# Sparse attention: scores of a head pair by 64-row halves, keys stored without the zeros

## The chip, the cores and the metric

The kernel runs on one core of one Trainium2 chip. The metric is the device time of one execution in microseconds. The kernel before takes 1622.97 us (median of 3 runs, 1621.4 to 1623.26).

## The reference

The program computes two stacked blocks of a small network on 256 tokens of width 1024, in fp32. The first block has an HGRN2 mixer, an attention mixer and two feed-forward layers; the second has a short convolution, a sparse attention mixer and four feed-forward layers. The change lies in the sparse attention alone. Cut to what matters there:

```
q = rmsnorm(x @ w_q)                        # 16 heads of 64, in 4 groups of 4 heads
k_cmp, v_cmp, k_sel, v_sel, k_win, v_win    # one head of 64 per group and branch
for each group g, each of its heads h:
    o_cmp = softmax(q[h] k_cmp[g]^T / 8, blocks that end at or before t) v_cmp[g]   # 15 compressed keys
    o_sel = softmax(q[h] k_sel[g]^T / 8, keys <= t) v_sel[g]
    o_win = softmax(q[h] k_win[g]^T / 8, keys <= t) v_win[g]
    out[h] = gate0 * o_cmp + gate1 * o_sel + gate2 * o_win
y = concat(out) @ w_o
```

With 256 tokens every block of 64 is selected and the window of 512 covers everything, so the selected and the window branch are both plain causal attention over 256 keys, with keys and values of their own.

## The kernel before, in words

All large products are split: a weight chunk arrives by DMA in `raw`, ScalarE rounds it to `hi` (`split_one`, L362) and VectorE writes the rest to `lo` (L363); TensorE adds three products per pair (L550, L571, L597). Almost the whole program is this stream of matmuls of 256 columns.

The sparse attention has three parts. `Sparse.__init__` makes the buffers that outlive a stage: GpSimd writes the zeros of `kbd`, `kcbd` and `vcbd` (L1102 to L1106). `project` makes keys and values from the shared projection; `key_t` (L1196) transposes the normalised keys of one branch on TensorE, two banks of PSUM for the two halves of the tokens, and each bank is written to `kbd` in two parts, rows 0 to 63 by ScalarE (L1206) and rows 64 to 127 by VectorE (L1207). `compress` does the compressed keys and ends with two ScalarE instructions into `kcbd` (L1284). `attend` (L1289) is the attention itself.

The queries of one pair of heads stand in 128 partitions: head 0 of the pair in partitions 0 to 63, head 1 in 64 to 127. `kbd` is block diagonal: in rows 0 to 63 the keys stand in the first half of the columns and zeros in the second, in rows 64 to 127 the other way round. One fp32 product over all 128 rows thus gives the scores of both heads side by side. A causal mask is added by one more matmul, identity times mask, in fp32r (one instruction, where an fp32 product is two, each a weight load and a matmul).

`pair(i)` (L1327), for eight pairs, has three stages, separated by `yield`. Stage 1 takes four PSUM banks of the pool `acc` (it has four in all): `pa` holds the scores of tokens 0 to 127 on the first 128 keys (two branches, two heads: four blocks of 128), `pb` and `pc` those of tokens 128 to 255 on all 256 keys (one branch each, two heads), `pd` the compressed scores (four blocks of 64). VectorE then takes the row maxima (four `tensor_reduce`, L1351), ScalarE the exponentials with row sums (twelve, L1354), in the order `pa`, `pb`, `pc`, `pd`, and VectorE the reciprocals, the gates and three products (L1357 to L1368). Stage 2 transposes the result (14 transposes, L1377 to L1386, pool `wk`) and copies it out. Stage 3 multiplies by the values (L1390 to L1398): one product on the whole array, then eight on halves of 64 columns, the two heads in turn, and splits the output into `zh`, `zl` (L1400).

`attend` interleaves `queries(g)`, stages of `pair(i)` and `out(k)` (the output projection, which needs all four `acc` banks) by a list written out by hand (L1418 to L1427). `queries(1)` uses two `acc` banks too. The order in which each engine then executes is made when the program is built, from dependences and free buffers: in the trace instructions of several pairs stand mixed on one engine.

Of the kernel before, what the change touches and what calls it, by code (L numbers as in the profile page):

```python
# [271 lines left out]
def nsa_masks():  # L272

    t = np.arange(P)[:, None]
# [3 lines left out]
    return np.concatenate([causal] + [c for c in cmp for _ in range(2)], axis=1).astype(np.float32)  # L278
# [813 lines left out]
class Sparse:  # L1092
    def __init__(self, net, pool):
# [3 lines left out]
        self.kbd = pool.tile([P, 2, 4, 2, T], F32, name="kbd")  # L1097
        self.v = pool.tile([P, 2, 2, T], F32, name="v_sw")
        self.kcbd = pool.tile([P, 4, P], F32, name="kcbd")
        self.vcbd = pool.tile([P, 4, P], F32, name="vcbd")  # L1100
        nc.scalar.dma_start(self.c, net.aps["nsa_c"])
        nc.gpsimd.memset(self.kbd[0:64, :, :, 1, :], 0.0)  # L1102
        nc.gpsimd.memset(self.kbd[64:P, :, :, 0, :], 0.0)
        for t in (self.kcbd, self.vcbd):
            nc.gpsimd.memset(t[0:64, :, 64:P], 0.0)
            nc.gpsimd.memset(t[64:P, :, 0:64], 0.0)  # L1106
# [89 lines left out]
    def key_t(self, s, kn):  # L1196
# [3 lines left out]
        for i in range(2):  # L1200
# [5 lines left out]
            nc.scalar.activation(self.kbd[0:64, br, :, 0, c], ps[0:64], AF.Copy, scale=gain[0:64])  # L1206
            nc.vector.tensor_scalar(self.kbd[64:P, br, :, 1, c], ps[64:P], gain[64:P], None, ALU.mult)  # L1207


    def compress(self):  # L1210
# [8 lines left out]
        for s in range(2):  # L1219
# [69 lines left out]
    def attend(self, norm, post):  # L1289
# [7 lines left out]
        causal = masks[:, :P]  # L1297
# [29 lines left out]
        def pair(i):  # L1327
            g, pr = i // 2, i % 2
            q = q_t[g][:, pr, :]
            pa, pb, pc, pd = [net.acc.tile([P, 512], F32, tag="acc", name=net.name("nl")) for _ in range(4)]  # L1330
            t0, t1 = q[:, 0:P], q[:, P:T]
# [227 lines left out]
```

## Time and profile before

| | |
|---|---|
| median of 3 runs | 1622.97 us (1621.4 to 1623.26) |
| profiled execution, own time | 1622.46 us |
| its span, first to last instruction | 1620.6 us |
| TensorE matmul busy | 1602.0 us, 99% |
| VectorE, ScalarE, GpSimd busy | 1127.2, 853.3, 53.2 us |
| mean granted TensorE clock | 0.999 |

Busy times are those of the profiled execution. A matmul's recorded end is modelled, so the records of matmuls that follow each other overlap: the cost of one is read from the distance between starts, not from its duration. `attend` lies between about 1318 and 1435 us of the span; its tiles in the profile are `nl` (scores; one name for `pa` to `pd`), `nmx` (maxima), `e` (exponentials), `nt` (transposes), `no` (product with the values).

### The profile page before, as it was taken

How to read it: one execution, taken by the hardware profiler on the slowest of the kernel's cores; microseconds unless marked ns; L12 is line 12 of the kernel's file. 1: busy time of each engine (PE TensorE's matmuls, PEld its weight loads, DVE VectorE, ACT ScalarE, POOL GpSimd, SP SyncE). 2: the span in 40 equal slices, each digit the busy share in tenths (PEclk: the TensorE clock that was granted, in tenths of full speed). 3: DMA queues.
4: the chain of work that ended last, by engine and by line, in shares of the span. 5: the costliest groups of instructions: out<-in, count | busy, mean ns of one | idle time of the engine just before them, and what ended most of it. 6: DMA issues, size and time to landing. Idle time of an engine off the chain costs nothing.

```text
span 1620.6 us, 32338 instructions
## 1 busy us (share of the span) xinstructions
PE 1602.0 (99%) x13704; PEld 1574.4 (97%) x13704; DVE 1127.2 (70%) x1657; ACT 853.3 (53%) x1392; POOL 53.2 (3%) x50
## 2 busy tenths in 40 slices
PE   8999999999999999999999999999999999999999
PEld 8999999999999999999999999999999996799999
DVE  6878866676586667866686866668666668776664
ACT  7674544455554446544454544455545557654442
POOL 0000100000000000000000100001000011000000
PEclk9999999999999999999999999999999999999999
DMA  8325455455445544654555555546554641045451
GB/s 311 130 94 183 176 187 204 179 192 190 143 187 182 205 182 157 231 207 184 201 190 186 200 191 194 197 157 234 183 210 181 237 167 49 29 161 208 180 207 51
DMA packets 43565, 289.09 MB, mean 178 GB/s; under 512 B 4851, under 2 KB 7580, under 8 KB 9244
## 3 DMA queue, kind: packets, MB, share of 16 engines
q1 hardware_dynamic: 42784, 286.48, 48.5%
q8 instruction: 107, 1.75, 0.4%
q10 hardware_dynamic: 636, 0.55, 0.1%
q14 instruction: 38, 0.31, 0.1%
HBM read 284.93 MB, written 1.06 MB: 176 GB/s over the span
## 4 chain that ended last, share of the span: by engine, by line
PE 84%; issue 10%; DVE 3%; POOL 1%; ACT 1%; DMA 0%; SPq 0%; DVEq 0%; POOLq 0%; ACTq 0%
PE pj L550 51%; PE dn L597 26%; PE pn L571 3%; PE nl L1332 1%; PE no L1332 1%; POOL hms L1131 1%; DVE lo L363 1%; PE ph L1237 1%; DVE xl L430 0%; POOL r L514 0%; DVE h L617 0%; DMA h<-x_t 0%; DVE e L1368 0%; PE mo L1043 0%; DVE e L466 0%
## 5 line engine op out<-in xcount | busy, mean ns | idle before, releaser
L363 DVE TENSOR_TENSOR lo<-raw,hi 128x1024 fp32r<-128x1024 f32 (+2 forms) x537 | 653.3, 1222 | 276.4 <-ACT hi L362 275.0
L362 ACT ACTIVATE hi<-raw 128x1024 fp32r<-128x1024 f32 (+2 forms) x537 | 562.0, 1055 | 470.9 <-PE pj L550 389.9
L550 PE MATMUL pj<-xh,hi 128*128 128x256 f32 x2656 | 738.7, 278 | 0.1
L550 PE MATMUL pj<-xl,hi 128*128 128x256 f32 x2656 | 735.5, 277 | 0.3 <-DVE xl L430 0.3
L550 PE MATMUL pj<-xh,lo 128*128 128x256 f32 x2656 | 734.9, 277 | 0.1
L550 PEld LDWEIGHTS pj<-xl,hi 128*128 128x128 f32 x2656 | 498.8, 188 | 1.4 <-DVE xl L430 0.8
L550 PEld LDWEIGHTS pj<-xh,hi 128*128 128x128 f32 x2656 | 498.9, 188 | 1.1 <-ACT xh L429 0.5
L550 PEld LDWEIGHTS pj<-xh,lo 128*128 128x128 f32 x2656 | 498.6, 188 | 0.4 <-DVE lo L363 0.3
L597 PE MATMUL dn<-zh,hi 128*128 128x256 f32 x1312 | 363.4, 277 | 0.0
L597 PE MATMUL dn<-zh,lo 128*128 128x256 f32 x1312 | 362.7, 276 | 0.0
L597 PE MATMUL dn<-zl,hi 128*128 128x256 f32 x1312 | 362.6, 276 | 0.0
L597 PEld LDWEIGHTS dn<-zh,hi 128*128 128x128 f32 x1312 | 246.4, 188 | 0.4 <-issue 0.2
L597 PEld LDWEIGHTS dn<-zl,hi 128*128 128x128 f32 x1312 | 246.3, 188 | 0.1
L597 PEld LDWEIGHTS dn<-zh,lo 128*128 128x128 f32 x1312 | 246.3, 188 | 0.0
L434 ACT ACTIVATE zh<-ft 128x256 fp32r<-128x256 f32 x132 | 54.7, 417 | 155.4 <-DVE ft L634 155.4
L631 DVE TENSOR_TENSOR ft<-pj,rbc 128x512 f32<-128x512 f32 x132 | 90.7, 690 | 51.1 <-PE pj L550 50.5
L435 DVE TENSOR_TENSOR zl<-ft,zh 128x256 fp32r<-128x256 f32 x132 | 55.7, 424 | 54.8 <-ACT zh L434 54.8
L571 PE MATMUL pn<-hi,xh 128*128 128x256 f32 (+1 forms) x256 | 73.7, 289 | 1.0 <-DVE e L1143 1.0
L571 PE MATMUL pn<-hi,xl 128*128 128x256 f32 (+1 forms) x256 | 72.9, 285 | 0.0
L571 PE MATMUL pn<-lo,xh 128*128 128x256 f32 (+1 forms) x256 | 72.6, 284 | 0.0
L632 ACT ACTIVATE ft<-ft 128x256 f32<-128x256 f32 x132 | 52.8, 402 | 9.9 <-DVE ft L631 9.7
L634 DVE TENSOR_TENSOR ft<-ft 128x256 f32<-128x256 f32 x132 | 54.9, 418 | 1.3 <-ACT ft L632 1.2
(236 smaller groups left out, 1144.6 us busy)
## 6 DMA issues: line engine op xcount, KB each, us to landing
raw<-wts SPq DMA_DIRECT2D x263, 1024.0 KB, 4.8
raw<-wts SPq DMA_DIRECT2D x4, 1072.0 KB, 5.0
h<-x_t SPq DMA_DIRECT2D x4, 256.0 KB, 4.8
hank<-bias_d SPq DMA_DIRECT2D x1, 1024.0 KB, 8.3
out_dram<-h SPq DMA_DIRECT2D x4, 256.0 KB, 2.1
kk<-lsum SPq DMA_DIRECT2D x1, 576.0 KB, 8.1
raw<-wts SPq DMA_DIRECT2D x2, 256.0 KB, 4.5
raw<-wts SPq DMA_DIRECT2D x1, 512.0 KB, 6.0
```

What stands on the lines that cost most here:

```text
L362: self.nc.scalar.activation(hi[:, p], src[:, p], AF.Copy)
L363: self.nc.vector.tensor_sub(lo[:, p], src[:, p], hi[:, p].bitcast(F32))
L434: self.nc.scalar.activation(hi, src, AF.Copy)
L435: self.nc.vector.tensor_sub(lo, src, hi.bitcast(F32))
L550: nc.tensor.matmul(o, a[:, c:c + P], b[k], start=(k == 0 and m == 0 and q == 0), stop=(k == KT - 1 and q == 2), skip_group_check=True)
L571: nc.tensor.matmul(o, a[k][:, i * P:(i + 1) * P], b[:, kk * ncol:(kk + 1) * ncol], start=(k == 0 and q == 0 and (i == 0 or banks == 2)), s ...
L597: nc.tensor.matmul(o, a[:, c:c + P], x, start=(j == 0 and m == 0 and q == 0), stop=(j == self.n - 1 and q == 2), skip_group_check=True)
L631: nc.vector.tensor_mul(t, ps, state["rb"])
L632: nc.scalar.activation(t[:, :T], t[:, :T], AF.Silu)
L634: nc.vector.tensor_mul(t[:, :T], t[:, :T], t[:, T:])
L1131: nc.gpsimd.tensor_tensor(ms[:, :n], ms[:, :n], net.nhalf[:, :n], ALU.pow)
L1332: mm = lambda o, a, b, st, sp: nc.tensor.matmul(o, a, b, start=st, stop=sp, skip_group_check=True)
```

## The change

The keys are stored once, in both halves of the partitions, without zeros: `k2[P, 4, 2, T]` (group, branch, key) takes the place of `kbd`, `kc2[P, 4, 64]` that of `kcbd`; the zeros are no longer written. The projection already makes the keys twice (`scaled2`), so one instruction over 128 partitions fills both halves: in `key_t` ScalarE does the first half of the tokens, VectorE the second; in `compress` one ScalarE instruction does both.

In `pair` each product runs over 64 rows of the array, one per head: `u` is the head, `c` its 64 partitions. Each head has banks of its own: `pa[u]` holds tokens 0 to 127 (two branches, 256 columns) and both compressed blocks (2 times 64 columns); `pb[u]` holds tokens 128 to 255 (two branches, 512 columns). The masks follow all products. There are six reductions instead of four, head 0 first; the exponentials keep their order (causal blocks of tokens 0 to 127, of 128 to 255, compressed), which now goes back and forth between the two heads' banks.

```diff
-            for br in range(2):
-                mm(pa[:, br * T:(br + 1) * T], t0, self.kbd[:, br, g, :, 0:P], br == 0, False)
-            mm(pa, identr, causal.unsqueeze(1).to_broadcast([P, 4, P]), False, True)
-            for br, x in enumerate((pb, pc)):
-                mm(x, t1, self.kbd[:, br, g, :, :].rearrange("p a t -> p (a t)"), True, False)
-                mm(x.rearrange("p (a t) -> p a t", a=2)[:, :, P:], identr, causal.unsqueeze(1).to_broadcast([P, 2, P]),
+            for u, c in enumerate(half):
+                mm(pa[u][:, :T], q[c, t0], self.k2[c, g, :, 0:P], True, False)
+            for u, c in enumerate(half):
+                mm(pb[u], q[c, t1], self.k2[c, g, :, :].rearrange("p b t -> p (b t)"), True, False)
+            for i_, t in enumerate((t0, t1)):
+                for u, c in enumerate(half):
+                    mm(pa[u][:, T + i_ * 64:T + i_ * 64 + 64], q[c, t], self.kc2[c, g, :], False, False)
+            for u in range(2):
+                mm(pa[u][:, :384], identr, masks, False, True)
+            for u in range(2):
+                mm(pb[u].rearrange("p (a t) -> p a t", a=2)[:, :, P:], identr, masks[:, :T].rearrange("p (a t) -> p a t", a=2),
                    False, True)
-            mm(pd[:, 0:P], t0, self.kcbd[:, g, :], True, False)
-            mm(pd[:, P:T], t1, self.kcbd[:, g, :], False, False)
-            mm(pd[:, :T], identr, masks[:, P:], False, True)
...
-            for src, c, n in ((pa, 0, 4), (pb, 4, 2), (pc, 6, 2), (pd[:, :T], 8, 4)):
-                nc.vector.tensor_reduce(mx[:, c:c + n], src.rearrange("p (h k) -> p h k", h=n), AX.X, ALU.max,
-                                        negate=True)
+            for u in range(2):
+                for src, c in ((pa[u][:, :T], 0), (pb[u], 4), (pa[u][:, T:384], 8)):
+                    nc.vector.tensor_reduce(mx[:, c + u:c + 4:2], src.rearrange("p (h k) -> p h k", h=2), AX.X, ALU.max,
+                                            negate=True)
...
-            nc.scalar.activation(self.kbd[0:64, br, :, 0, c], ps[0:64], AF.Copy, scale=gain[0:64])
-            nc.vector.tensor_scalar(self.kbd[64:P, br, :, 1, c], ps[64:P], gain[64:P], None, ALU.mult)
+            if i:
+                nc.vector.tensor_scalar(self.k2[:, :, br, c], ps, gain, None, ALU.mult)
+            else:
+                nc.scalar.activation(self.k2[:, :, br, c], ps, AF.Copy, scale=gain)
...
-            for o in (0, 64):
-                nc.scalar.activation(self.kcbd[o:o + 64, :, o:o + 64], pt[o:o + 64, :, o:o + 64], AF.Copy,
-                                     scale=self.col(C_KN)[o:o + 64])
+            nc.scalar.activation(self.kc2, pt[:, :, 0:64], AF.Copy, scale=self.col(C_KN))
```

## Rows read from the trace of the kernel before

**Rows 1.** The page's first lines: the span, and each engine's busy time in us, its share of the span and its instructions.

```profile
span 1620.6 us, 32338 instructions
PE 1602.0 (99%) x13704; PEld 1574.4 (97%) x13704; DVE 1127.2 (70%) x1657; ACT 853.3 (53%) x1392; POOL 53.2 (3%) x50
```

**Rows 2.** Busy times by stretch inside `attend`: from:to in us, its length, then busy us (and instructions) of PE, PEld, DVE, ACT, POOL, the granted clock, the DMA share and GB/s.

```profile
1343.00:1412.00 69.00, 65.93 (x428) 49.00 (x429) 54.31 (x127) 51.65 (x227) 4.12 (x2) 0.98 0.08 30
...
1384.00:1410.00 26.00, 25.74 (x185) 18.46 (x187) 21.66 (x49) 19.41 (x88) 0.00 (x0) 1.00 0.00 1
...
1344.00:1348.00 4.00, 4.00 (x17) 3.39 (x18) 2.41 (x5) 3.27 (x17) 0.00 (x0) 0.58 0.39 166
```

**Rows 3.** The chain that ended last, from 1318 to 1425 us: its shares by line, and one of its pieces (start us, us, what).

```profile
by line: PE nl L1332 15.4%; PE no L1332 12.6%; PE dn L597 10.3%; POOL hms L1131 8.6%; PE pn L571 6.9%; DVE lo L363 5.6%; DVE e L1368 3.9%; PE nt L1377 3.3%; DVE xl L430 3.1%; PE nt L1382 3.0%; issue 2.9%; DVE nmx L1351 2.8%; PE nt L1378 2.7
...
1391.94 3.61 PE nl L1332 x16
```

**Rows 4.** TensorE's timeline over the scores of pair 6, which stand here in one piece: start us, us, engine, line, out<-in, rows*columns of the array, moving operand, how many were merged.

```profile
1391.77 1.03 PE L1332 MATMUL nl<-kbd,qt 128*128 128x256 f32 x4
1392.45 0.58 PE L1332 MATMUL nl<-masks,identr 128*128 128x512 f32 x1
1392.87 1.02 PE L1332 MATMUL nl<-kbd,qt 128*128 128x512 f32 x2
1393.33 0.68 PE L1332 MATMUL nl<-masks,identr 128*128 128x256 f32 x1
1393.85 1.02 PE L1332 MATMUL nl<-kbd,qt 128*128 128x512 f32 x2
1394.30 0.68 PE L1332 MATMUL nl<-masks,identr 128*128 128x256 f32 x1
1394.82 0.61 PE L1332 MATMUL nl<-kcbd,qt 128*128 128x128 f32 x4
1395.18 0.36 PE L1332 MATMUL nl<-masks,identr 128*128 128x256 f32 x1
```

**Rows 5.** The same timeline, just after: one whole product with the values (`no`), and the first row of the next.

```profile
1395.38 0.59 PE L1332 MATMUL no<-yb,vcbd 128*128 128x256 f32 x2
1395.91 0.65 PE L1332 MATMUL no<-ya,v_sw 128*64 128x256 f32 x4
1396.39 0.39 PE L1332 MATMUL no<-yb,v_sw 128*64 128x128 f32 x4
1396.61 0.60 PE L1332 MATMUL no<-ya,v_sw 128*64 128x256 f32 x4
1397.04 0.39 PE L1332 MATMUL no<-yb,v_sw 128*64 128x128 f32 x4
1397.36 0.70 PE L1332 MATMUL no<-yb,vcbd 128*128 128x256 f32 x2
```

**Rows 6.** Groups of VectorE instructions between 1339 and 1420 us, shapes apart: count | busy us, mean ns | idle time before them and what ended it. First the maxima, then the three products.

```profile
L1351 DVE TENSOR_REDUCE nmx<-nl 128x2 f32<-128x512 f32 x16 | 10.6, 675 | 0.4 <-PE nl L1332 0.3
L1351 DVE TENSOR_REDUCE nmx<-nl 128x4 f32<-128x512 f32 x8 | 5.4, 678 | 3.5 <-PE nl L1332 3.3
L1351 DVE TENSOR_REDUCE nmx<-nl 128x4 f32<-128x256 f32 x8 | 3.3, 415 | 0.4 <-PE nl L1332 0.4
...
L1368 DVE TENSOR_TENSOR e<-e,ncf 128x1024 f32<-128x1024 f32 x8 | 9.7, 1217 | 0.0
L1368 DVE TENSOR_TENSOR e<-e,ncf 128x512 f32<-128x512 f32 x8 | 5.5, 684 | 0.0
L1368 DVE TENSOR_TENSOR e<-e,ncf 128x256 f32<-128x256 f32 x8 | 3.3, 417 | 0.0
```

**Rows 7.** ScalarE's timeline: the first and the last of pair 0's twelve exponentials, then the last of pairs 1, 4 and 7.

```profile
1344.73 0.37 ACT L1354 ACTIVATE e<-nl,nmx 128x128 f32<-128x128 f32 x1 [4.21 <-DVE nmx L1351]
...
1348.78 0.37 ACT L1354 ACTIVATE e<-nl,nmx 128x64 f32<-128x64 f32 x1
...
1356.79 0.33 ACT L1354 ACTIVATE e<-nl,nmx 128x64 f32<-128x64 f32 x1
...
1386.95 0.33 ACT L1354 ACTIVATE e<-nl,nmx 128x64 f32<-128x64 f32 x1
...
1411.30 0.35 ACT L1354 ACTIVATE e<-nl,nmx 128x64 f32<-128x64 f32 x1
```

**Rows 8.** TensorE's timeline: the first scores of pair 2 and of pair 5.

```profile
1353.24 0.60 PE L1332 MATMUL nl<-kbd,qt 128*128 128x256 f32 x2
...
1381.11 1.03 PE L1332 MATMUL nl<-kbd,qt 128*128 128x256 f32 x4
```

**Rows 9.** TensorE's timeline: the scores of pair 0 that go to `pc`; in brackets the idle time before and what ended it.

```profile
1343.82 1.30 PE L1332 MATMUL nl<-kbd,qt 128*128 128x512 f32 x2 [1.90 <-DVE qn L1138]
```

**Rows 10.** The instructions that write the keys (duration min/median/max in ns, first and last start in us), a wait of TensorE in that stage (us in total, times, longest), and GpSimd's timeline at the zeros and after them.

```profile
L1206 ACT ACTIVATE kbd<-kt,nsa_c x4: 667/677/683, 1110.9 to 1125.6; 64x512 f32<-64x512 f32 x4
...
L1207 DVE TENSOR_SCALAR kbd<-kt,nsa_c x4: 753/756/757, 1115.0 to 1126.5; 64x512 f32<-64x512 f32 x4
...
PEld pn L571 <- ACT kbd L1206: 1.2, 1, 1.2
...
898.39 1.81 POOL L1102 MEMSET kbd<- 64x2048 f32 x1 [47.91 <-DVE zl L435]
...
906.44 1.31 POOL L466 TENSOR_TENSOR e<-e 128x512 f32<-128x512 f32 x1 [3.01 <-issue]
```

More of the change, by code (lines that the diff above doesn't have):

```diff
@@ L277, in nsa_masks @@
     cmp = [np.where((n < 15) & (16 * n + 31 <= t + P * i), 0.0, NEG) for i in range(2)]
-    return np.concatenate([causal] + [c for c in cmp for _ in range(2)], axis=1).astype(np.float32)
+    return np.concatenate([causal, causal] + cmp, axis=1).astype(np.float32)
 def pack_rel(inputs):
@@ L1096, in __init__ @@
         self.c = pool.tile([P, N_C], F32, name="nsa_c")
-        self.kbd = pool.tile([P, 2, 4, 2, T], F32, name="kbd")
+        self.k2 = pool.tile([P, 4, 2, T], F32, name="k2")
         self.v = pool.tile([P, 2, 2, T], F32, name="v_sw")
-        self.kcbd = pool.tile([P, 4, P], F32, name="kcbd")
+        self.kc2 = pool.tile([P, 4, 64], F32, name="kc2")
         self.vcbd = pool.tile([P, 4, P], F32, name="vcbd")
         nc.scalar.dma_start(self.c, net.aps["nsa_c"])
[L1102 to L1106, printed above, removed]
+        nc.gpsimd.memset(self.vcbd[0:64, :, 64:P], 0.0)
+        nc.gpsimd.memset(self.vcbd[64:P, :, 0:64], 0.0)
         self.hq = pool.tile([P, 1], F32, name="hq")
@@ L1296, in attend @@
         nc.vector.tensor_copy(identr, net.ident)
-        causal = masks[:, :P]
         q_t, gates, z = {}, {}, {}
@@ L1329, in pair @@
             q = q_t[g][:, pr, :]
-            pa, pb, pc, pd = [net.acc.tile([P, 512], F32, tag="acc", name=net.name("nl")) for _ in range(4)]
-            t0, t1 = q[:, 0:P], q[:, P:T]
+            pa = [net.acc.tile([P, 512], F32, tag="acc", name=net.name("nl")) for _ in range(2)]
+            pb = [net.acc.tile([P, 512], F32, tag="acc", name=net.name("nl")) for _ in range(2)]
+            half = [slice(u * 64, u * 64 + 64) for u in range(2)]
+            t0, t1 = slice(0, P), slice(P, T)
             mm = lambda o, a, b, st, sp: nc.tensor.matmul(o, a, b, start=st, stop=sp, skip_group_check=True)
-            for br in range(2):
-                mm(pa[:, br * T:(br + 1) * T], t0, self.kbd[:, br, g, :, 0:P], br == 0, False)
-            mm(pa, identr, causal.unsqueeze(1).to_broadcast([P, 4, P]), False, True)
-            for br, x in enumerate((pb, pc)):
-                mm(x, t1, self.kbd[:, br, g, :, :].rearrange("p a t -> p (a t)"), True, False)
-                mm(x.rearrange("p (a t) -> p a t", a=2)[:, :, P:], identr, causal.unsqueeze(1).to_broadcast([P, 2, P]),
+            for u, c in enumerate(half):
[9 more added lines that the diff above has]
+                mm(pb[u].rearrange("p (a t) -> p a t", a=2)[:, :, P:], identr, masks[:, :T].rearrange("p (a t) -> p a t", a=2),
                    False, True)
-            mm(pd[:, 0:P], t0, self.kcbd[:, g, :], True, False)
-            mm(pd[:, P:T], t1, self.kcbd[:, g, :], False, False)
-            mm(pd[:, :T], identr, masks[:, P:], False, True)
             mx = net.sp.tile([P, 12], F32, tag="nmx", name=net.name("nmx"))
@@ L1346, in pair @@
             xa, xb = net.e4(), net.e4()
-            parts = [(pa[:, j * P:(j + 1) * P], xa[:, j * P:(j + 1) * P]) for j in range(4)]
-            parts += [((pb, pc)[j // 2][:, (j % 2) * T:(j % 2 + 1) * T], xb[:, j * T:(j + 1) * T]) for j in range(4)]
-            parts += [(pd[:, j * 64:(j + 1) * 64], xa[:, 512 + j * 64:512 + (j + 1) * 64]) for j in range(4)]
-            for src, c, n in ((pa, 0, 4), (pb, 4, 2), (pc, 6, 2), (pd[:, :T], 8, 4)):
-                nc.vector.tensor_reduce(mx[:, c:c + n], src.rearrange("p (h k) -> p h k", h=n), AX.X, ALU.max,
-                                        negate=True)
+            parts = [(pa[j % 2][:, (j // 2) * P:(j // 2 + 1) * P], xa[:, j * P:(j + 1) * P]) for j in range(4)]
+            parts += [(pb[j % 2][:, (j // 2) * T:(j // 2 + 1) * T], xb[:, j * T:(j + 1) * T]) for j in range(4)]
+            parts += [(pa[j % 2][:, T + (j // 2) * 64:T + (j // 2 + 1) * 64], xa[:, 512 + j * 64:512 + (j + 1) * 64])
+                      for j in range(4)]
+            for u in range(2):
+                for src, c in ((pa[u][:, :T], 0), (pb[u], 4), (pa[u][:, T:384], 8)):
+                    nc.vector.tensor_reduce(mx[:, c + u:c + 4:2], src.rearrange("p (h k) -> p h k", h=2), AX.X, ALU.max,
+                                            negate=True)
             for j, (src, dst) in enumerate(parts):
```

## The prediction

> **What bounds the kernel now.** I read the page's head first: TensorE is busy 99% of the span, VectorE 70%, ScalarE 53% [rows 1], so only what shortens TensorE's stream, or makes it wait, can count. But a share of the whole span says little of one stage, so I next read busy times by stretch inside the attention [rows 2]. From 1343 to 1412 us, where the eight pairs' scores lie, TensorE is busy 65.93 of 69 us, VectorE 54.31, ScalarE 51.65: TensorE leads, the others are not far behind. From 1384 to 1410 it is 25.74 of 26 against 21.66 and 19.41. The chain of waits over 1318 to 1425 us [rows 3] then says how much of that stretch hangs on the scores: 15.4% of 107 us, that is 16.5 us. As one pair's scores in one piece take 3.61 us [rows 3], eight take 28.9 us; 57% of them stand on the chain. The rest of the chain is other TensorE work and, up to about 1384, maxima, products and the query scaling on VectorE and GpSimd.
>
> **The scores on TensorE.** From the starts in [rows 4, 5]: two fp32 products of 256 columns and a mask of 512 take 1.10 us (1391.77 to 1392.87), a product of 512 and a mask of 256 take 0.98 (twice), two products of 128 and a mask of 256 take 0.56; together 3.61. An fp32 product is two instructions. The first two differ by 256 mask columns, so these cost 0.12 us, and an fp32 instruction of 256 columns costs (1.10 - 0.24)/4 = 0.215 us. After the change the number of columns is the same: products of 2 x 256, 2 x 512 and 4 x 64 against 2 x 256, 2 x 512 and 2 x 128. Were the halves to run one after the other nothing would be won. All hangs on two halves running side by side.
>
> The trace has no product on 64 rows. The nearest is that on 64 columns, the product with the values [rows 5]. One takes 1.98 us (1395.38 to 1397.36). One after the other its instructions would take 2 x 0.215 on the whole array and 8 x 0.215 + 8 x 0.108 on halves, 3.01 us; with the halves side by side 0.43 + 1.29 = 1.72. So they do run side by side, and the 0.26 us left over is what going to halves and back costs. I take the same for rows. Then a pair's scores cost: tokens 0 to 127, 2 x 0.215 = 0.43; tokens 128 to 255, 0.86; the compressed ones 0.22 if columns decide and 0.36 if the weight load does (four instructions with 128-column weights take 1394.82 to 1395.18), I take 0.29; masks 1280 columns, 0.60; the change of shape 0.26. Sum 2.44 us, 1.17 less than 3.61; for eight pairs 9.4 us. The bounds: 1.10 to 1.24 less if the pair stays in one piece; if another pair's transposes come between its parts, as at 1353.24, where only two of pair 2's four instructions are merged [rows 8], each further change costs another 0.26.
>
> The Trainium skill, TensorEngine Tiling (Array Packing), section Key Properties, says that a change of tiling mode drains TensorE. The 0.26 us above is what that takes here, and by this rule a pair in four pieces would gain only about 0.4 us.
>
> With 57% of the scores on the chain, 9.4 us become 5.3 us.
>
> **What it adds on VectorE.** Today's maxima are three of 512 elements and one of 256 per pair, 19.3/8 = 2.41 us [rows 6]. The six new ones are two each of 256, 512 and 128 elements. None of 128 is shown; the line through 415 ns and 677 ns gives 0.28 us. Sum 0.83 + 1.35 + 0.57 = 2.75 us, 0.34 more per pair, 2.7 in all. The maxima stand on the chain with 2.8% of 107 us, 3.0 of 19.3 us [rows 3, 6]; so 0.4 us of it counts. Bounds 0 (VectorE has 14.7 us to spare in the 69) and 2.7.
>
> **What it moves: the banks.** This is the cost that is hard to see in the diff. Today `pa` comes free after four exponentials, and pair i+1's first product can start while pair i's others run: pair 2 starts at 1353.24 although pair 1's last exponential is at 1356.79; pair 5 at 1381.11, pair 4's last at 1386.95 [rows 7, 8]. After the change both `pa` banks also hold the compressed scores, whose exponentials come last, so tokens 0 to 127 of the next pair wait for the eleventh and twelfth exponential. Behind that product TensorE queues the pair's masks, then the next transposes; for the masks wait VectorE's maxima and ScalarE's exponentials. The scores also come out later within a pair: the first masked bank today 1.10 us after the start, then 0.43 + 0.86 + 0.29 + 0.18 + about 0.13 for the change of shape = 1.9.
>
> The ring that this closes: scores 1.9; a maximum 0.42, then the first exponential; the second needs head 1, so four maxima, 0.42 + 0.68 + 0.28 + 0.42 = 1.8; eleven exponentials at (1348.78 - 1344.73)/11 = 0.37, 4.05 [rows 7]. Sum 7.75 us. VectorE's three products of the pair before, 18.5/8 = 2.3 us [rows 6], with small ones around them, start when the ring restarts and stick out of the 1.9 by 0.4 to 1.0. So 8.15 to 8.75, middle 8.45. Today the last exponentials of pair 0 and pair 7 are 1411.30 - 1348.78 = 62.5 us apart, 8.93 per pair. Seven rounds at 8.45 would be 59.2, 3.3 us less. That is below the 5.3 - 0.4 = 4.9 us by the chain, so the ring, not TensorE, sets what is won. The output projection needs all four banks, so it too starts when pair 7's last exponentials are done.
>
> Pair 0 is a case by itself: its last two banks come from `queries(1)`, and TensorE waits 1.90 us for them [rows 9], after which the granted clock is 0.58 over 4 us [rows 2]. After the change 0.86 + 0.24 + 0.26 = 1.36 us of work is left behind that wait if the rest goes ahead, 2.0 if not, against 0.98 + 0.56 today: -0.3 to +0.8 at that clock. I take 0.
>
> **The other edits** count nothing. The keys: two ScalarE and two VectorE instructions of 0.68 and 0.76 us go [rows 10]; TensorE's one wait there, 1.2 us, is put down to a ScalarE instruction on the keys, but a VectorE one that I leave as it is ended its matmul's wait too; bounds -1.2 and 0. The zeros end long before GpSimd's next instruction, which waited 3.01 us for something else [rows 10]. The compressed keys lie beside a feed-forward layer on TensorE.
>
> **Sum.** 1622.46 - 3.3 = 1619.2 by the profiled execution; it is 0.5 us under the median of the runs, by which it would be 1619.7. I forecast 1619.5 us; the likeliest case alone has 1617 to 1621.5.
>
> **Rivals.**
> *All of TensorE's gain comes through* (0.20). For it: 25.74 of 26 us busy, so late there every microsecond of the scores counts, and the planner may let `pb`, free four exponentials earlier than `pa`, go first, which loosens the ring. Then 9.4 - 0.4 and some loss early, 5.5 to 9: 1613.5 to 1617, middle 1615.5. Against it: VectorE has 54.31 + 2.7 of 69 us already.
>
> *The ring costs more than the array gives: slower* (0.27). If a round takes over 8.93 us, the pairs come later than today. VectorE executes in order; a copy of 0.68 or a split of the weights between two maxima lengthens the round by itself. At 9.5 us seven rounds are 66.5, 4.0 us more: 1626.6. For it: pairs 2 and 5 start 3.6 and 5.8 us before their predecessor's last exponential, which is gone. Against it: several rounds today are longer than 8.93 anyway (pair 1 to pair 4: (1386.95 - 1356.79)/3 = 10.1), so there is slack in them. It decides from 8.93 us. The Trainium skill, TensorEngine Tiling (Array Packing), section PSUM Bottleneck, warns of this: tiling speeds up TensorE but not the evacuation of PSUM. No row here shows the evacuation as the bound yet.
>
> *The 64-row halves don't run side by side* (0.11). Then the products cost 0.86 + 1.72 + 0.43, with masks and change of shape 3.87 us, 0.26 more than today, and the ring gets 1.3 us longer, 9.75: seven rounds are 5.7 us more than today, less what slack hides: about 1627. For it: no row shows a row half. Against it: column halves do it for the same type.
>
> **Chances.** The forecast has 0.42. Less than 0.2% (3.2 us) cannot be told from no change. Faster by more: the second case and half of the first, 0.20 + 0.22 = 0.42. Slower by more: 0.16 of the ring's 0.27 and 0.09 of the last. Same: the rest, 0.33. For 8 in 10 the range goes from 1613.5, the full gain, to 1627, the two slower cases' middles.
>
> **What would show it.** The chain's piece of a pair's scores: about 2.4 us instead of 3.61, with two 64-row matmuls starting together; 3.9 refutes the halves. The distance from pair 0's last exponential to pair 7's: 59 us by the forecast, 62.5 or more by the ring. VectorE about 2.7 us busier there, TensorE with idle time before the scores that ends on an exponential. The forecast is wrong if that distance shrinks by over 5 us or grows.

## The result, and the profile after

The changed kernel takes 1640.68 us (median, 1639.64 to 1642.07), the kernel before, run beside it, 1622.64 us: a ratio of 1.0116, 95% interval 1.0105 to 1.0127. It is 18 us slower. The profiled execution's span is 1640.3 us. The page's head, to be laid beside [rows 1]:

```profile
span 1640.3 us, 32410 instructions
...
PE 1611.3 (98%) x13736; PEld 1580.6 (96%) x13736; DVE 1128.1 (69%) x1671; ACT 851.4 (52%) x1389; POOL 48.1 (3%) x46
```

19.7 us of span more, of which TensorE is busy for only 9.3: the rest is idle time. Where it lies is told by ScalarE's last exponentials of pair 0 and of pair 7, and by the output projection's first product behind them (the first fence ScalarE's timeline, the second TensorE's):

```profile
1352.33 0.34 ACT L1359 ACTIVATE e<-nl,nmx 128x64 f32<-128x64 f32 x1
...
1431.32 0.37 ACT L1359 ACTIVATE e<-nl,nmx 128x64 f32<-128x64 f32 x1
```

```profile
1430.19 0.38 PE L597 MATMUL dn<-zh,hi 128*128 128x256 f32 x1 [1.97 <-ACT e L1359]
```

From pair 0's last to pair 7's it is 79.0 us, against 62.5 in [rows 7]: 16.5 of the 19.7 us. Pair 0's last is 3.55 us later than before, and from pair 7's to the end of the span it is 209.0 us, before 209.3. The mean round from pair to pair is 79.0/7 = 11.3 us.

Busy times of the same part, then the chain over 1318 to 1445 us, its shares and some of its pieces (as [rows 2, 3]):

```profile
1343.00:1430.00 87.00, 73.17 (x444) 52.90 (x444) 56.15 (x142) 50.43 (x217) 4.37 (x3) 0.82 0.07 25
```

```profile
by line: PE nl L1333 20.0%; PE no L1333 12.6%; ACT e L1359 11.1%; PE dn L597 9.8%; DVE lo L363 5.7%; POOL hms L1129 5.3%; DVE nmx L1356 4.0%; issue 3.9%; PE pn L571 3.5%; PE nt L1382 2.9%; PE nt L1383 2.7%; DVE xl L430 2.6%; DVE h L617 2.0%
...
1356.67 2.88 ACT e L1359 x14
1359.60 5.58 PE nl L1333 x17
1365.18 1.88 PE no L1333 x18
...
1368.87 2.88 ACT e L1359 x14
1371.80 4.70 PE nl L1333 x17
...
1395.61 3.83 PE no L1333 x18
1399.44 2.68 PE nl L1333 x20
...
1406.50 5.60 PE nl L1333 x17
```

TensorE was busy 96% of this stage before and is busy 84% now, at a mean granted clock of 0.82 instead of 0.98. The chain has a member that it did not have: the exponentials, 11.1% of 127 us. Read its first pieces in a row: seven exponentials (2.88 us; each is two instructions), then a pair's scores (5.58), a product with the values (1.88), and soon the next pair's exponentials. On this chain they stand one behind another. The waits of that stretch, grouped, say the same: VectorE waits for the exponentials' row sums, TensorE for exponentials ahead of its scores. In the trace of before no group of scores that waits for `e` is among the largest:

```profile
DVE nsm L1362 <- ACT e L1359: 16.9, 7, 3.5
...
PEld nl L1333 <- ACT e L1359: 6.0, 4, 3.1
```

The array does what the change says. Pair 5's scores on TensorE's timeline, in one piece:

```profile
1399.38 1.56 PE L1333 MATMUL nl<-k,qt 64*128 64x256 f32 x8
1400.77 0.56 PE L1333 MATMUL nl<-kc,qt 64*128 64x64 f32 x8
1401.26 0.87 PE L1333 MATMUL nl<-masks,identr 128*128 128x384 f32 x4
1401.96 0.27 PE L1382 MATMUL nt<-ident,e 128*128 128x128 f32 x1
```

1401.96 - 1399.38 = 2.58 us instead of 3.61 [rows 3, 4]: the 64-row halves run side by side. The pieces of pairs 2, 3 and 6 on the chain took 5.58, 4.70 and 5.60 us for the same work, at a mean granted clock of 0.51, 0.64 and 0.50 and with the halves in part apart. A product with the values took 1.88 us at full clock (1365.18) and 3.83 us at 0.54 (1395.61).

### The profile page after: what moved, and what is told of

Same layout as the page of the kernel before. It is cut to its first block, busy times and chain, and to the rows that moved or that the text cites. A ratio compares the mean times of both kernels' runs of the same rounds, so it can differ in the third digit from the quotient of the medians.

```text
span 1640.3 us, 32410 instructions
## 1 busy us (share of the span) xinstructions
PE 1611.3 (98%) x13736; PEld 1580.6 (96%) x13736; DVE 1128.1 (69%) x1671; ACT 851.4 (52%) x1389; POOL 48.1 (3%) x46
## 3 DMA queue, kind: packets, MB, share of 16 engines
q8 instruction: 107, 1.75, 0.4%
HBM read 284.93 MB, written 1.06 MB: 174 GB/s over the span
## 4 chain that ended last, share of the span: by engine, by line
PE 84%; issue 10%; DVE 3%; ACT 1%; POOL 1%; DMA 0%; SPq 0%; DVEq 0%; POOLq 0%; ACTq 0%
PE pj L550 50%; PE dn L597 26%; PE pn L571 2%; PE nl L1333 2%; PE no L1333 1%; ACT e L1359 1%; DVE lo L363 1%; PE ph L1237 1%; POOL hms L1129 1%; DVE xl L430 0%; POOL r L514 0%; DVE h L617 0%; DVE nmx L1356 0%; DMA h<-x_t 0%; PE mo L1043 0%
```

## The experiments

Time is the median; the ratio is to the kernel before, run on the same chip in the same job. "Distance" is that from pair 0's last exponential to pair 7's in the profiled execution (before 62.5, changed 79.0 us). The kernel before took 1621.2 to 1622.3 us beside these runs, so small differences between runs are read from how far each is above it. In 10, 13 and 15 the profiled execution was 1.9, 3.4 and 2.5 us below the median; the distance is that execution's.

| | us | ratio (95%) | distance |
|---|---|---|---|
| 1 changed order and banks, products on 128 rows | 1641.39 | 1.0123 (1.0108 to 1.0138) | 77.2 |
| 2 before's banks, halves for tokens 128 to 255 | 1625.56 | 1.0023 (1.0014 to 1.0033) | 65.6 |
| 3 changed, with matmuls that fill the idle time | 1651.11 | 1.0183 (1.0168 to 1.0198) | 87.2 |
| 4 changed, masks behind their products | 1639.54 | 1.0112 (1.0097 to 1.0127) | 77.2 |
| 5 before, banks held | 1625.64 | 1.0024 (1.0014 to 1.0034) | 65.2 |
| 6 before, masks late | 1627.10 | 1.0031 (1.0020 to 1.0043) | 66.2 |
| 7 before, both | 1637.16 | 1.0089 (1.0074 to 1.0104) | 74.9 |
| 8 as 4, maxima in order of need | 1637.34 | 1.0091 (1.0074 to 1.0108) | 77.5 |
| 9 as 8, compressed maxima early | 1634.93 | 1.0084 (1.0069 to 1.0099) | 72.8 |
| 10 as 9, exponentials bank by bank | 1634.92 | 1.0080 (1.0065 to 1.0095) | 71.6 |
| 11 as 10, products on 128 rows | 1625.34 | 1.0021 (1.0012 to 1.0031) | 64.6 |
| 12 changed, maxima and exponentials bank by bank | 1640.88 | 1.0119 (1.0104 to 1.0134) | 80.3 |
| 13 changed, wide banks first | 1633.30 | 1.0075 (1.0057 to 1.0093) | 70.0 |
| 14 as 13, products on 128 rows | 1627.12 | 1.0034 (1.0022 to 1.0047) | 65.9 |
| 15 as 2, the two wide banks freed together | 1624.64 | 1.0014 (1.0005 to 1.0023) | 62.5 |

### Is it the halves, the banks, or the clock?

**1.** The kernel before's keys and 128-row products, in the changed kernel's banks, with its masks, maxima and order of exponentials.

```diff
...
-                mm(pa[u][:, :T], q[c, t0], self.k2[c, g, :, 0:P], True, False)
+                mm(pa[u][:, :T], q[:, t0], self.kbd[:, :, g, u, 0:P], True, False)
...
-                mm(pb[u], q[c, t1], self.k2[c, g, :, :].rearrange("p b t -> p (b t)"), True, False)
+                mm(pb[u], q[:, t1], self.kbd[:, :, g, u, :], True, False)
...
-                    mm(pa[u][:, T + i_ * 64:T + i_ * 64 + 64], q[c, t], self.kc2[c, g, :], False, False)
+                    mm(pa[u][:, T + i_ * 64:T + i_ * 64 + 64], q[:, t], self.kcbd[:, g, u * 64:u * 64 + 64], False, False)
```

> This has the changed kernel's banks, masks, maxima and order of exponentials, but every product on all 128 rows with the block-diagonal keys, as before. Theory of the banks (what a pair's exponentials hold back is the next pair's scores): clearly slower than before, 1635 to 1650 us, the scores 3.6 us in one piece at full clock and TensorE waiting for exponentials ahead of them. Theory of the array (64-row halves, or the changes of shape they bring, cost the time): as before, 1620 to 1626 us.

The whole loss is there without a single 64-row product. Its busy times over the stretch, and its largest waits of the scores:

```profile
1343.00:1430.00 87.00, 72.78 (x464) 54.84 (x465) 57.70 (x148) 52.36 (x228) 3.62 (x3) 0.97 0.07 24
```

```profile
PEld nl L1333 <- ACT e L1359: 7.7, 4, 3.1
...
PE nl L1333 <- ACT e L1359: 6.8, 4, 2.8
```

The granted clock is 0.97 (changed kernel: 0.82), and the time is the changed kernel's. So the loss does not need the low clock: TensorE waits for the exponentials either way. It does not follow that the low clock of the changed kernel is free. TensorE is busy for 73.17 us there and for 72.78 here, though its halves should take less. Pair 6 shows it, first in the changed kernel, then in run 1: the first product, the first mask (TensorE's timelines), and the busy times over the pair's scores.

```profile
1406.50 1.25 PE L1333 MATMUL nl<-k,qt 64*128 64x256 f32 x3 [2.85 <-ACT e L1359]
...
1410.66 1.44 PE L1333 MATMUL nl<-masks,identr 128*128 128x384 f32 x4
...
1406.50:1412.10 5.60, 5.60 (x21) 4.03 (x22) 3.21 (x9) 1.85 (x11) 0.00 (x0) 0.50 0.00 0
```

```profile
1405.10 0.70 PE L1333 MATMUL nl<-kbd,qt 128*128 128x256 f32 x2 [2.85 <-ACT e L1359]
...
1408.28 1.15 PE L1333 MATMUL nl<-masks,identr 128*128 128x384 f32 x4
...
1405.10:1409.43 4.33, 4.33 (x21) 3.27 (x22) 2.68 (x8) 1.84 (x11) 0.00 (x0) 1.00 0.00 0
```

Both wait 2.85 us for an exponential. Then the first mask comes 4.16 us behind the first product with halves at clock 0.50, 3.18 us with whole products at 1.00. In the changed kernel's pairs 4 and 5, at full clock and with all banks free, it comes after 1.88. So on pairs like this the halves' gain is gone, with the clock at half. What the changed kernel would take at full clock no run shows.

**2.** The other way round: the kernel before's banks and order, halves only for tokens 128 to 255 (`pb` for head 0, `pc` for head 1). The keys are kept both ways.

```diff
...
-            for br, x in enumerate((pb, pc)):
-                mm(x, t1, self.kbd[:, br, g, :, :].rearrange("p a t -> p (a t)"), True, False)
+            for u, x in enumerate((pb, pc)):
+                c = slice(u * 64, u * 64 + 64)
+                mm(x, q[c, P:T], self.k2[c, g, :, :].rearrange("p b t -> p (b t)"), True, False)
...
```

> The opposite corner: the banks of before in their order, with the scores of tokens 128 to 255 by 64-row halves (bank pb for head 0, pc for head 1); tokens 0 to 127 and the compressed scores stay on 128 rows. A pair's scores should take about 3.0 us instead of 3.61. Theory of the banks: no slower than before, 1617 to 1623 us. Theory of the array: slower than before by about half of what the change lost, 1628 to 1635 us.

Neither. `pb` and `pc` come free one at a time, and the order made when the program is built issues each product for its own bank. Only pair 1 has its two wide halves side by side (1.13 us for both); elsewhere they stand apart (pair 4: 1374.35 and 1381.54) or one behind the other (pair 6: 2.01 us).

**3.** Fourteen matmuls of identity and masks ahead of each pair's products, into a bank of `wk`.

```diff
+            if i:
+                fill = net.wk.tile([P, 512], F32, tag="wk", name=net.name("fill"))
+                for _ in range(14):
+                    nc.tensor.matmul(fill[:, :384], identr, masks, start=True, stop=True, skip_group_check=True)
```

> The changed kernel with 14 masks-times-identity matmuls of 384 columns (about 2.5 us at full clock) into a spare bank ahead of the products of pairs 1 to 7; nobody reads them. Theory of the clock (the idle time halves TensorE's clock, and that is a good part of the loss): granted clock over 0.95 between 1343 and 1430 us and the time 3 to 9 us below the changed kernel's 1640.7, although TensorE gets 17 us more to do. If the clock is a by-product and the ring of waits sets the time: 1640 to 1650 us.

The clock comes back in part, to 0.92 over 1343 to 1430 us and not over 0.95, and the time goes up by 10 us, 1 us beyond the second range. The added matmuls themselves stand on the chain (9.1% of it from 1318 to 1455 us, some 12 us): what TensorE does ahead of the scores lengthens the round. What the lost clock costs the changed kernel this run can't tell.

**4.** The changed kernel, each masks product behind its own bank pair's products (`pa`, then `pb`).

> The changed kernel with each mask right behind its products: pa and its masks complete before pb starts. One more change of shape per pair (0.26 us), but the first maxima can start about 1 us earlier. If the late first masked bank is a large part of the ring: 2 to 7 us below 1640.7. If not, within 2 us of it.

Within 2 us of the changed kernel. Alone, the masks' place is not it.

### What of the order makes the loss: on the kernel before

**5.** One line of the kernel before: an order of the exponentials in which every bank keeps one for the end.

```diff
-            for j, (src, dst) in enumerate(parts):
+            for j, (src, dst) in ((j, parts[j]) for j in (0, 1, 2, 4, 6, 8, 9, 10, 3, 5, 7, 11)):
```

> The kernel before with one line changed: the twelve exponentials of a pair are ordered so that each of its four banks has one of its exponentials among the last four (0, 1, 2, 4, 6, 8, 9, 10, 3, 5, 7, 11 in place of 0 to 11). Nothing else differs: same products, maxima, tiles. Theory (banks held): what the change costs is that a pair's banks come free late in its row of exponentials, so that the next pair's products, maxima and exponentials stand behind one another; then this kernel loses most of what the changed kernel loses: 1632 to 1640 us, and from the last exponential of the first pair to that of the last 72 to 78 us in place of 62.5. Rival (the new shapes cost: six maxima in place of four, two heads interleaved, merged tiles): a mere order of exponentials costs under 3 us, 1620 to 1624 us, and the distance stays at 62 to 65 us.

1625.64, nearer the rival. Holding all four banks to the last third (the changed kernel holds two of them so long) costs 4 us by itself and not 15.

**6, 7.** The masks of `pa`, `pb`, `pc` behind all products; then both edits together.

```diff
-            mm(pa, identr, causal.unsqueeze(1).to_broadcast([P, 4, P]), False, True)
...
             mm(pd[:, P:T], t1, self.kcbd[:, g, :], False, False)
+            mm(pa, identr, causal.unsqueeze(1).to_broadcast([P, 4, P]), False, True)
...
```

> The kernel before with its three masks of pa, pb and pc moved behind all its products (the order of products is kept). Its banks, maxima and exponentials stay as they are. Theory (no overlap inside a pair): pa's maximum and first exponentials wait for all four banks to be free and written, so the time goes well up: 1629 to 1638 us, distance 70 to 77 us in place of 62.5. Rival (the release of the banks alone, or the shapes): under 4 us, up to 1625 us.

> The run above (the kernel before with masks behind all products) and the order of exponentials that holds all four banks to the last third (0, 1, 2, 4, 6, 8, 9, 10, 3, 5, 7, 11), which alone cost 4 us. Theory (both together make the pairs stand strictly one behind another, and each covers for the other when alone): 1635 to 1645 us, distance 75 to 85 us, as the changed kernel and its variant on 128 rows. Rival (costs merely add): the run above plus 3 to 5 us.

Late masks cost 5 us alone, between the two ranges; 4 and 5 together are 15. The clock has a part in the 15: the one execution of 7 whose mean clock was 0.999, as in 6, took 1634.30 us, 12 above the kernel before and still more than 4 and 5 added. This is the interaction the theory asked for, on a kernel with the old tiles, four maxima and full products, and its chain has the changed kernel's face (19.3, 11.2 and 4.4% against 20.0, 11.1 and 4.0% for scores, exponentials and maxima):

```profile
by line: PE nl L1332 19.3%; PE dn L597 12.7%; ACT e L1355 11.2%; PE no L1332 9.7%; POOL hms L1131 6.6%; DVE lo L363 4.8%; PE pn L571 4.7%; DVE nmx L1352 4.4%; issue 2.8%; DVE xl L430 2.6%; PE nt L1378 2.2%; DVE h L617 2.0%; PE nt L1383 1.9%
```

With banks freed early, the next pair's scores run under this pair's exponentials, even if they come out late; with masks early, this pair's exponentials run under its own later products, even if the banks are held. Either overlap is nearly enough. Without both, scores, maxima and exponentials of one pair after another form one line.

### Mending the order in the changed kernel

**8.** As 4, and the maxima in the order in which the exponentials need them.

```diff
-            for u in range(2):
-                for src, c in ((pa[u][:, :T], 0), (pb[u], 4), (pa[u][:, T:384], 8)):
+            for u, src, c in ((0, pa[0][:, :T], 0), (1, pa[1][:, :T], 0), (0, pb[0], 4), (1, pb[1], 4),
+                              (0, pa[0][:, T:384], 8), (1, pa[1][:, T:384], 8)):
```

> The changed kernel (64-row halves, its banks, its order of exponentials) with two things put back together: each bank pair's masks stand right behind its own products (pa, then pb), and the six maxima are in the order in which the exponentials need them (pa, pa, pb, pb, then the two compressed ones) in place of head by head. Theory (no overlap inside a pair: with the masks at the end and the maxima head by head, the second exponential waits for the whole pair's products and four of the six maxima, so products, maxima and exponentials stand one behind another): the distance from the first pair's last exponential to the last pair's falls from 79 to 66 to 70 us and the time to 1625 to 1632 us. Rival (the release of the banks sets the round, two after seven and eight exponentials and two after eleven and twelve, which stays as it was): 1636 to 1641 us, distance 75 to 79 us.

My theory failed: 1637.34, distance 77.5. Pair 1 shows why (VectorE's timeline, then ScalarE's):

```profile
1352.68 0.42 DVE L1357 TENSOR_REDUCE nmx<-nl 128x2 f32<-128x256 f32 x1 [1.05 <-PE nl L1333]
...
1355.31 2.01 DVE L1357 TENSOR_REDUCE nmx<-nl 128x2 f32<-128x256 f32 x5
```

```profile
1357.15 0.37 ACT L1360 ACTIVATE e<-nl,nmx 128x128 f32<-128x128 f32 x1 [0.55 <-DVE nmx L1357]
```

The first exponential needs only the first maximum, which is done at 1353.10. It starts at 1357.15, 0.03 us behind the fifth, `pa[0]`'s compressed one (1356.84 to 1357.12, inside the second row). Pair 7 has the same: `pa[0]`'s compressed maximum ends at 1424.29, the first exponential starts at 1424.38. The first exponential of a bank waits for VectorE's last maximum of that bank, though both only read it. The Trainium skill, PSUM — Partial Sum Buffer, section "PSUM bank collisions raise a hardware error", states that the compiler back end's scheduler adds a dependency between two engines on the same bank and quadrant, "reads and writes alike". The trace agrees, with the 0.03 us. The changed kernel has it too: in pairs 3, 4, 6 and 7 the first exponential starts 0.09 to 0.12 us behind the third maximum, `pa[0]`'s compressed one. The kernel before has one maximum per bank, so nothing of this shows there.

**9.** As 8, each compressed maximum right behind its bank's other one.

```diff
-            for u, src, c in ((0, pa[0][:, :T], 0), (1, pa[1][:, :T], 0), (0, pb[0], 4), (1, pb[1], 4),
-                              (0, pa[0][:, T:384], 8), (1, pa[1][:, T:384], 8)):
+            for u, src, c in ((0, pa[0][:, :T], 0), (0, pa[0][:, T:384], 8), (1, pa[1][:, :T], 0),
+                              (1, pa[1][:, T:384], 8), (0, pb[0], 4), (1, pb[1], 4)):
```

> The kernel with masks behind their own products and six maxima in the order of need (1637.3 us), with one thing moved: each bank's compressed maximum stands right behind its other maximum (pa 0, its compressed, pa 1, its compressed, pb 0, pb 1). Exponentials in the changed kernel's order. In the traces the first exponential of a pair began 0.03 to 0.1 us behind the compressed maximum of its bank, wherever that stood in the order. Theory (an exponential waits until VectorE has read its whole bank): the exponentials of a pair then begin four maxima earlier, and the rows of twelve no longer stand as one block of 4.4 us: 1626 to 1632 us, distance 65 to 71 us in place of 77.5. Rival (that the banks come free late decides alone, two after seven and eight exponentials, two after eleven and twelve): 1635 to 1639 us, distance 75 to 79 us.

Pair 1's first exponential now starts at 1356.04, right behind the second maximum (1355.67 to 1355.95), and pair 7's at 1417.46, 0.03 us behind its second: the wait went where the bank's last maximum went. The distance falls by 4.7 us, between theory and rival; the time is at the rival's lower end, 13.4 us above the kernel before, where 8 was 15.1 above.

**10, 11.** As 9, exponentials bank by bank (`pa[0]`, `pa[1]`, `pb[0]`, `pb[1]`); then the same with 128-row products.

```diff
-            for j, (src, dst) in enumerate(parts):
+            for j, (src, dst) in ((j, parts[j]) for j in (0, 2, 8, 10, 1, 3, 9, 11, 4, 6, 5, 7)):
```

> The run above and the exponentials bank by bank as well (pa 0, pa 1, pb 0, pb 1), so that banks come free after 4, 8, 10 and 12 exponentials (the kernel before: after 4, 6, 8 and 12). Theory (late start of the exponentials inside a pair and late release of the banks together make the loss, and each covers for the other): with both undone 1621 to 1626 us, distance 62 to 66 us. Rival (a pair of halves needs two free banks, so a release one by one still holds the products up): 1629 to 1634 us, as the order with the wide banks first gave.

> The run above with the products on all 128 rows and the keys with zeros. Theory (halves are worth what they save only where both banks are free at once; else a half alone takes as long as a full product and costs two changes of shape): 0 to 6 us below the run above, as with the wide banks first. Rival (halves side by side save 1.1 us per pair on the path): 3 to 8 us above the run above.

10 missed its theory and lies 1 us above its rival's range, no faster than 9. With 128-row products the mended order takes 16 of 1's 20 us away (1641.39 to 1625.34). With halves it takes away only 5 of 18 (18.0 us above the kernel before, then 13.4), and 10 is 9.6 us above 11, more than I had expected. TensorE's timelines in pair 1, where both kernels have the same order, first 10, then 11:

```profile
1352.13 0.70 PE L1333 MATMUL nl<-k,qt 64*128 64x256 f32 x2
1352.66 0.55 PE L1333 MATMUL nl<-kc,qt 64*128 64x64 f32 x4
1353.14 0.44 PE L1333 MATMUL nl<-masks,identr 128*128 128x384 f32 x1
1353.51 1.12 PE L1333 MATMUL nl<-k,qt 64*128 64x512 f32 x2
1354.57 0.38 PE L1333 MATMUL nl<-masks,identr 128*128 128x256 f32 x1
1354.88 1.12 PE L1333 MATMUL nl<-k,qt 64*128 64x512 f32 x2
```

```profile
1351.37 0.59 PE L1333 MATMUL nl<-kbd,qt 128*128 128x256 f32 x2
1351.80 0.55 PE L1333 MATMUL nl<-kcbd,qt 128*128 128x64 f32 x4
1352.16 0.42 PE L1333 MATMUL nl<-masks,identr 128*128 128x384 f32 x1
1352.42 1.02 PE L1333 MATMUL nl<-kbd,qt 128*128 128x512 f32 x2
1352.88 0.68 PE L1333 MATMUL nl<-masks,identr 128*128 128x256 f32 x1
1353.40 1.02 PE L1333 MATMUL nl<-kbd,qt 128*128 128x512 f32 x2
```

Banks that come free one by one get one half at a time. A half alone, with its mask, takes 1.38 us (1352.13 to 1353.51) against 1.05 for the whole array, and the wide one 1.37 against 0.98: +0.33 and +0.39, for two banks of each kind 1.44 us per pair. Side by side, as in 10's pair 4, both wide banks with masks take about 1.6 us against 2.1. So the sign of the change on TensorE hangs on whether two banks are free at once. In 10 the wide halves of pairs 3, 4 and 5 start together, those of pairs 1, 2, 6 and 7 apart, and the scores take 26.9% of its chain from 1318 to 1437 us, 32 us, against 21.7% of 11's from 1318 to 1430, 24 us.

A second part of the 9.6 us goes with the clock: over 1340 to 1420 us it is 0.94 in 10 and 0.98 in 11, which is 3.2 us of full speed. Behind pair 4's scores TensorE waits for the queries in both:

```profile
1388.78 0.45 PE L1317 MATMUL pqt<-ident,qn 128*128 128x128 f32 x1 [2.50 <-DVE qn L1136]
1389.02 0.42 PE L1383 MATMUL nt<-ident,e 128*128 128x128 f32 x1
1389.23 0.42 PE L1384 MATMUL nt<-ident,e 128*128 128x128 f32 x1
```

```profile
1385.64 0.30 PE L1320 MATMUL pqt<-ident,qn 128*128 128x128 f32 x1 [1.72 <-DVE qn L1138]
1385.78 0.27 PE L1383 MATMUL nt<-ident,e 128*128 128x128 f32 x1
1385.89 0.27 PE L1384 MATMUL nt<-ident,e 128*128 128x128 f32 x1
```

Behind the wait a transpose takes 0.21 us from start to start in 10, where the granted clock is 0.50 from 1388.27 to 1391.69, and 0.11 in 11. The chain of 10 passes through these transposes, so the clock is on its path there; what it adds over the whole stage is not shown.

**12.** The changed kernel with 10's order of maxima and exponentials, its masks behind all products.

> The changed kernel with maxima and exponentials bank by bank (as two runs above), its masks left behind all products. It tells what the place of the masks is worth once the order is mended: theory (late masks alone cost the kernel before 5 us): 4 to 7 us above the run with masks behind their own products. Rival (the masks' place matters only with banks held late): within 2 us of it.

6 us above 10, about what late masks cost in 6. With the masks alone (4) or this order alone (12) the changed kernel gained nothing; with both (10) it did.

**13, 14.** The two banks of tokens 128 to 255 first throughout (products, masks, maxima, exponentials); then with 128-row products.

```diff
...
+            for j, (src, dst) in ((j, parts[j]) for j in (4, 6, 5, 7, 0, 2, 8, 10, 1, 3, 9, 11)):
```

> The changed kernel with another order inside a pair: the two banks of tokens 128 to 255 first (allocation, products, their masks, maxima, their four exponentials), then the two banks of tokens 0 to 127 with the compressed scores. Two banks come free together after four of the twelve exponentials, the other two after eight and twelve (in the changed kernel two after seven and eight, two after eleven and twelve). Theory (banks held): some 1 us earlier products per round, and the masks no longer at the end, so 1.5 to 2.5 us less per round on seven rounds: 1623 to 1630 us, distance 62 to 69 us in place of 79. Rival (new shapes, or the maxima, cost): 1637 to 1642 us.

> The run above (two banks of tokens 128 to 255 first) with the products on all 128 rows and the keys with the block diagonal's zeros, as the kernel before has them. It tells what the 64-row halves are worth in that order. Theory (banks held, and the halves' saving of about 1.1 us per pair counts wherever the products stand on the path): 4 to 8 us above the run above. Rival (the halves' saving is hidden, as it was between the changed kernel and its variant on 128 rows): within 2 us of the run above.

With 128-row products most of the loss goes with this order too (5.9 of 1's 20.2 us above the kernel before are left), with halves a third (12.0 of 18.0 are left). Again the halves are the slower ones, by 6 us; I had expected the reverse. The profiled executions, both at clock 0.999, are only 2.8 us apart (1629.87 and 1627.07 us); the other three with halves had 0.995 to 0.997 and took 3 to 5 us more than the profiled one, so here, too, a part goes with the clock.

**15.** As 2, the exponentials of `pb` and `pc` alternating, so that the two banks come free closer together.

```diff
-            for j, (src, dst) in ((j, parts[j]) for j in (0, 1, 2, 3, 4, 6, 5, 7, 8, 9, 10, 11)):
+            for j, (src, dst) in enumerate(parts):
```

> The mixed kernel (the kernel before's banks, 64-row halves for tokens 128 to 255 alone) with its exponentials of these two banks alternating, so that the two banks come free 0.4 us apart in place of 0.7 to 4. Theory (the halves gained nothing there because they were issued apart): more pairs have them side by side (1.1 us for both in place of 1.9), and the time is 1620 to 1624 us against 1625.6. Rival (what it costs is the later release of the first bank and the change of array shape): 1625 to 1628 us.

Three pairs have their wide halves fully side by side, where 2 has one. The distance is that of before, 62.5, in a profiled execution of 1622.11 us. The median, between theory and rival, is 0.14% above before, with an interval just clear of none (1.0005 to 1.0023): with halves that run together in three pairs it is still no faster than before, and its interval overlaps that of 2.

## Why the prediction was wrong

**The scores on TensorE: right.** 2.44 us forecast, 2.58 measured, halves side by side. What I didn't price was the half alone. The sum had a case of pairs in pieces (0.26 us per further change of shape), but took from [rows 5] that halves go side by side whenever both are issued. The value product has one bank for both halves; a row half has a bank of its own, and banks come free one by one. Alone, a half is slower than the whole array by 0.33 to 0.39 us. The Trainium skill, TensorEngine Tiling (Array Packing), section Key Properties, says that a change of mode drains TensorE; the rows agree: in 11 a mask's record begins 0.46 us behind its product's (1352.42, 1352.88), in 10 1.06 us behind (1353.51, 1354.57).

**The maxima: right.** Forecast 2.75 us per pair. Measured (VectorE's groups over 1343 to 1430 us) 10.8 + 6.7 + 4.5 = 22.0 us in eight pairs, 2.75:

```profile
L1356 DVE TENSOR_REDUCE nmx<-nl 128x2 f32<-128x512 f32 x16 | 10.8, 680 | 0.1
...
L1356 DVE TENSOR_REDUCE nmx<-nl 128x2 f32<-128x256 f32 x16 | 6.7, 417 | 3.8 <-PE nl L1333 3.7
...
L1356 DVE TENSOR_REDUCE nmx<-nl 128x2 f32<-128x128 f32 x16 | 4.5, 280 | 0.0
```

**The banks: the step that failed.** It is the step from "Sum 7.75 us", with VectorE's products 8.45, to "Seven rounds at 8.45 would be 59.2, 3.3 us less"; measured were 79.0, 11.3 per round. The ring was the right mechanism, and its rival had the right sign, but the price was put against the mean of before and left terms out. From pair to pair, last exponential to last exponential on ScalarE's timeline:

| round | 1 | 2 | 3 | 4 | 5 | 6 | 7 |
|---|---|---|---|---|---|---|---|
| before, us | 8.0 | 9.4 | 7.0 | 13.8 | 6.7 | 5.9 | 11.7 |
| changed, us | 8.4 | 12.2 | 8.6 | 16.5 | 9.6 | 9.4 | 14.4 |

Rounds 1 and 3 came as forecast. But 8.93 is a mean of two long rounds and five of 5.9 to 9.4 us, 7.4 on average: a ring of 8.45 lengthens four of those five, and nothing in the sum shortens the long ones. At the forecast price for the five, with the two long ones as before, my estimate would be 5 x 8.45 + 25.6 = 67.8 us, 5.3 more than before and not 3.3 less.

The terms that fell: first, "scores 1.9". In pairs 4 and 5 `pa`'s first mask did follow 1.88 us behind the first product. In pairs 2, 3 and 6 it took 4.16, 3.85 and 4.16: the masks stand behind `pb`'s products, which wait for the last exponentials of the pair before (in pair 2 they start at 1361.35, 1.75 us behind the first product) and then run at the lower clock, for which the sum had no term. In pair 7, whose scores came in pieces, it took 8.05. With pair 1's 2.22 that is 26.2 us over seven rounds where the sum had 13.3: 12.9 of the 19.8 us that the rounds are longer than forecast. Second, "stick out by 0.4 to 1.0": once scores, maxima and exponentials stand in one line, other work that the engines execute in between (value products, copies, the queries' scaling) lengthens the line instead of lying under it. Between pair 2's first maximum (1364.64) and its second exponential (1369.22) lie 4.6 us, where I had allowed 1.8; pair 4's first product starts 5.3 us behind pair 3's last exponential (1381.51), and its first maximum 3.95 us behind its first mask (1388.67). In the other pairs the 1.8 was 1.7 to 2.2, and the exponentials took their 4.05. I also missed the wait for the bank's last maximum (8, 9).

That the release came after seven exponentials for the next pair's first product, and not after eleven or twelve as I assumed, was an error to the other side; it saved little, since `pb` waited.

**Pair 0 and the keys: too small.** I took 0 for both. Pair 0's last exponential is 3.55 us later. 0.44 us of it stands already at the first key transpose (1110.28 against 1109.84), ahead of the keys; the rest, 3.1 us, lies in keys and pair 0, outside my bounds (-1.2 to 0 and -0.3 to +0.8). Run 1, with full keys, has 1.9 us of the 3.55, so part of it is again the order; and the clock is at its lower level over pair 0 in the changed kernel (1344.55 to 1351.38), not in run 1.

**The rivals.** "The ring costs more than the array gives" was the case that came, at four times its size (18 us against 4.0), with both signs that I had named: the longer distance, and TensorE's idle time that ends on an exponential. Its argument against itself, slack in the rounds, was wrong: six of seven rounds grew by 1.6 to 3.4 us, the other by 0.4.

Three things stay open: why the mended order on 128 rows (11) is still 3.8 us above before, how much of 10's excess over 11 is the clock, and what the changed kernel would take at full clock.

## What to carry to other kernels

When a change repacks results into other PSUM banks, write down for each bank when its last reader is done and when its first reader can start, and walk two consecutive rounds through every engine's order; on the kernel before a late release cost 4 us and a late start 5, and both together 15. Price the new round against each round of before and not against their mean. Row halves of the array paid here only where both their banks were free at the same time; issued alone, each took longer than the product on the whole array. Group what one engine reads of a bank, since here the next engine started only when all of it had been read.

## What the runs showed of the hardware

Column halves in one bank [rows 5] and row halves in two behave alike once both are issued: 2.58 us for a pair's scores where the sum from the column halves gave 2.44. Not expected was the clock's part: in the changed kernel it stands at its lower level (1.2 of 2.4 GHz) for five stretches, 30.7 us in all between 1344 and 1413 us, where the kernel before and run 1 have one of 3.4 us. It is not idle time alone that tells where it falls: ahead of pair 6's scores TensorE waited 2.85 us for an exponential in the changed kernel and in run 1, and then had 0.50 in the one and 1.00 in the other. What decides it stays open. Run 1 shows that the loss comes without the low clock; where it does come, in pair 6, the scores take 5.60 us from first product to last mask, against 2.75 in pairs 4 and 5.
